# Row sums of a 64 MB tensor: the first group loaded as 4 and 12 rows, and a one-column copy ahead of the last sum

## The chip, the cores and the metric

One core of a Trainium2 chip. The time is device time in microseconds (us) of one execution; the profile's span is about 1.86 us shorter.

## The reference

```python
def setup_inputs():
    batch, seq, dim = 32, 512, 1024
    return {"x": np.random.randn(batch, seq, dim).astype(np.float32)}

def reference(x):
    return np.sum(x, axis=-1).astype(np.float32)
```

16,384 rows of 1,024 floats are summed: 67.11 MB read, 64 KB written.

## The kernel before

Each of the 128 partitions takes 128 rows, in 8 groups of 16. A full group's load gives a partition 16 rows that lie together in memory (64 KB). VectorE sums most rows. Towards the end ScalarE takes some rows of each load. The very last row comes in two pieces, of 560 and 464 columns: the sum of the first piece is written in front of the second, so that the second piece's instruction gives the row's whole sum. `hold` makes one instruction wait for another: the third load, and behind it all later loads, is issued only when the first sum is done.

```python
    last = J // BIG - 1                 # BIG = 16, J = 128
    FIRST = 7
    pieces = (560, 464)
    # ... pools: "in" has 3 buffers of one group each
        def halves(dst, src):           # sum of a row: left half + right half, accumulated
            n = src.shape[-1] // 2
            return nc.vector.tensor_tensor_reduce(
                out=src[:, :n], in0=src[:, :n], in1=src[:, n:], scale=1.0, scalar=0.0,
                op0=mybir.AluOpType.add, op1=mybir.AluOpType.add, accum_out=dst)
    # ... rows(t, a, n, j, n_act, pairs): loads n rows from row j of each partition's share, sums
    #     n - n_act of them on VectorE (one reduction, or `halves` row by row), n_act on ScalarE
        j = last * BIG
        t = inpool.tile([P, BIG * dim + 4], fp32)
        rows(t, 0, FIRST, j, 0)         # 7 rows of the last group come first
        first = sums_of[-1]
        for g in range(last):
            t = inpool.tile([P, BIG * dim + 4], fp32)
            if g < last - 1:
                load = rows(t, 0, BIG, g * BIG, 0)
            else:
                rows(t, 0, BIG, g * BIG, 7, pairs=True)
            if g == 1:
                hold(load, first, "no descriptors of later loads while the first ones start")
        t = inpool.tile([P, BIG * dim + 4], fp32)
        rows(t, FIRST, 6, j + FIRST, 2, pairs=True)
        two = rows(t, FIRST + 6, 2, j + FIRST + 6, 1, pairs=True)
        # ... the two pieces of the last row are loaded into `part` and `whole`
        hold(store(nc.scalar, 0, last), two, "its packets come behind those of the loads")
        halves(whole[:, :1], part)
        halves(sums[:, j : j + 1], whole)
        store(nc.sync, last, last + 1)
```

Of the kernel before, what the change touches and what calls it, by code (L numbers as in the profile page):

```python
# [118 lines left out]
@with_exitstack  # L119
def kernel(  # L120
    ctx: ExitStack,
    tc: tile.TileContext,
    x: bass.AP,
    out: bass.AP,
):
    nc = tc.nc
    nc.at_finalize(issue_first_load_at_entry)
    nc.at_finalize(order_waits)
    nc.at_finalize(wait_for_the_store_at_the_clear)
    fp32 = mybir.dt.float32  # L130
    P = 128
    batch, seq, dim = x.shape
    rows = batch * seq
    J = rows // P
    BIG = 16


    x_g = x.flatten_outer_dims().rearrange("(g p j) d -> g p j d", p=P, j=BIG)
    out_v = out.rearrange("b s -> (b s)").rearrange("(g p j) -> p g j", p=P, j=BIG)

    def rows_from(j, n):
        return x_g[j // BIG, :, j % BIG : j % BIG + n, :]



    last = J // BIG - 1
    FIRST = 7
    pieces = (560, 464)

    with (  # L150
        tc.tile_pool(name="in", bufs=3) as inpool,
        tc.tile_pool(name="unread", bufs=4, space=bass.MemoryType.PSUM) as upool,
        tc.tile_pool(name="stage", bufs=1) as stpool,
        tc.manual_schedule(),
    ):
        sums = stpool.tile([P, J], fp32)

        def vec(dst, src):
            return nc.vector.tensor_reduce(  # L159
                out=dst, in_=src, axis=mybir.AxisListType.X, op=mybir.AluOpType.add  # L160
            )

        def hold(inst, until, reason):
            tc.add_manual_dep(
                inst.ins,
                until.ins.name,
                mybir.DependencyInfo(mybir.DependencyClass.Sync, mybir.DependencyReason.DATA),
                reason=reason,
            )

        def halves(dst, src):
            n = src.shape[-1] // 2
            return nc.vector.tensor_tensor_reduce(  # L173
                out=src[:, :n],
                in0=src[:, :n],
                in1=src[:, n:],
                scale=1.0,
                scalar=0.0,
                op0=mybir.AluOpType.add,
                op1=mybir.AluOpType.add,  # L180
                accum_out=dst,
            )

        def act(dst, src, n):
            unread = upool.tile([P, dim], fp32)
            nc.scalar.activation(  # L186
                out=unread[:, :n],
                in_=src,
                func=mybir.ActivationFunctionType.Copy,
                accum_out=dst,  # L190
            )

        sums_of = []

        def rows(t, a, n, j, n_act, pairs=False):
            nv = n - n_act
            block = t[:, a * dim : (a + n) * dim].rearrange("p (n d) -> p n d", d=dim)
            load = nc.sync.dma_start(out=block, in_=rows_from(j, n))  # L198
            if pairs:
                for q in range(nv):  # L200
                    sums_of.append(halves(sums[:, j + q : j + q + 1], block[:, q, :]))
            else:
                sums_of.append(vec(sums[:, j : j + nv], block[:, :nv, :]))
            for q in range(nv, n):
                act(sums[:, j + q : j + q + 1], block[:, q, :], dim)
            return load

        def store(eng, g0, g1):
            return eng.dma_start(
                out=out_v[:, g0:g1],  # L210
                in_=sums[:, g0 * BIG : g1 * BIG].rearrange("p (g j) -> p g j", j=BIG),
            )


        j = last * BIG
        t = inpool.tile([P, BIG * dim + 4], fp32)
        rows(t, 0, FIRST, j, 0)
        first = sums_of[-1]
        for g in range(last):
            t = inpool.tile([P, BIG * dim + 4], fp32)  # L220
            if g < last - 1:
                load = rows(t, 0, BIG, g * BIG, 0)
            else:
                rows(t, 0, BIG, g * BIG, 7, pairs=True)
            if g == 1:
                hold(load, first, "no descriptors of later loads while the first ones start")

        t = inpool.tile([P, BIG * dim + 4], fp32)
        rows(t, FIRST, 6, j + FIRST, 2, pairs=True)
        two = rows(t, FIRST + 6, 2, j + FIRST + 6, 1, pairs=True)  # L230
        a = BIG - 1



        j += a
        c, width = pieces
        whole = t[:, a * dim + c : BIG * dim + 2]
        nc.vector.memset(whole[:, width + 1 :], 0.0)  # L238
        part = t[:, a * dim : a * dim + c]
        nc.sync.dma_start(out=part, in_=rows_from(j, 1)[:, 0, :c])  # L240
        nc.sync.dma_start(out=whole[:, 1 : width + 1], in_=rows_from(j, 1)[:, 0, c:])
        hold(store(nc.scalar, 0, last), two, "its packets come behind those of the loads")
        halves(whole[:, :1], part)
        halves(sums[:, j : j + 1], whole)
        store(nc.sync, last, last + 1)


# [28 lines left out]
```

## Time and profile before

| | before |
|---|---|
| time, median of the first 3 runs | 161.63 us (161.49 to 162.1) |
| span of the profile | 159.57 us |
| queue of the loads | 12 loads, busy 97.8% |
| VectorE, ScalarE busy | 76%, 7% |
| last load lands / last sum starts / last store issued | 157.51 / 157.57 / 158.01 us |

How to read it: the loads fill the span, so what can be gained is a quicker start of the stream, less overhead in it, or a shorter tail after the last landing. The lines are in the prediction. One view more, VectorE's timeline at the end of the kernel before (start, duration, engine, line, operation, operands): the first piece's sum (280 pairs), the read-out of its accumulator, and the second piece's sum (233 pairs).

```profile
156.97 0.45 DVE L173 CUSTOM_DVE_ANT_0 t<-t 128x280 f32<-128x280 f32 x1
157.34 0.08 DVE L173 DVE_READ_ACCUMULATOR2_ANT t<- 128x1 f32 x1
157.57 0.41 DVE L173 CUSTOM_DVE_ANT_0 t<-t 128x233 f32<-128x233 f32 x1
```

Between the read-out's end (157.42) and the start at 157.57 VectorE does nothing.

### The profile page before, as it was taken

The page shows a single profiled execution, that of the slowest core. Times are in us where ns is not written, and L with a number is a line of the kernel's source. Part 1 is how long each engine was busy: PE and PEld are TensorE (multiplying, and loading weights), DVE is VectorE, ACT ScalarE, POOL GpSimd, SP SyncE. Part 2 cuts the span into 40 slices and gives each one's busy share as a digit, 9 for nine tenths or more (in the row PEclk, how much of TensorE's full clock was granted, in tenths as well). Part 3 has the DMA queues.
Part 4 walks back from the last instruction along what each step waited for, and adds up shares of the span by engine and source line. Part 5 has one row for each costly group of instructions (what it writes and reads, how often), then busy time and mean ns, then how long its engine had stood idle before and what let it go on. Part 6 is the DMA issues. An engine that isn't in the chain of part 4 may idle for free.

```text
span 159.6 us, 134 instructions
## 1 busy us (share of the span) xinstructions
DVE 120.6 (76%) x40; ACT 11.9 (7%) x21; POOL 0.2 (0%) x4
## 2 busy tenths in 40 slices
DVE  0029600499995999779996899949999499994955
ACT  3000000000000000000000000000000000002993
POOL 0000000000000000000000000000000000000000
DMA  8899899799699699699699799998996996996994
GB/s 323 367 493 526 378 411 526 312 476 526 263 526 526 263 526 526 263 526 493 296 526 444 345 526 394 394 526 378 411 526 279 509 526 263 526 526 265 425 382 127
DMA packets 2784, 67.18 MB, mean 421 GB/s; under 512 B 1248, under 2 KB 1376, under 8 KB 1504
## 3 DMA queue, kind: packets, MB, share of 16 engines
q1 hardware_dynamic: 1872, 67.12, 97.8%
q10 hardware_dynamic: 912, 0.06, 0.4%
HBM read 67.11 MB, written 0.07 MB: 421 GB/s over the span
## 4 chain that ended last, share of the span: by engine, by line
DMA 71%; DVE 27%; SPq 1%; issue 0%; DVEq 0%
DMA t<-in_x_dram 71%; DVE sums L159 26%; SPq L198 0%; SPq L240 0%; DVE t L173 0%; DVEq L271 0%
## 5 line engine op out<-in xcount | busy, mean ns | idle before, releaser
L159 DVE TENSOR_REDUCE sums<-t 128x16 f32<-128x16384 f32 (+1 forms) x7 | 110.9, 15848 | 33.3 <-DMA t<-in_x_dram 33.3
L186 ACT ACTIVATE unread<-t 128x1024 f32<-128x1024 f32 x10 | 10.1, 1013 | 144.7 <-DMA t<-in_x_dram 144.7
L173 DVE CUSTOM_DVE_ANT_0 t<-t 128x512 f32<-128x512 f32 (+2 forms) x16 | 9.7, 656 | 4.0 <-DMA t<-in_x_dram 3.8
L186 ACT ACTIVATION_READ_ACCUMULATOR unread<-t 128x1 f32 x10 | 1.9, 187 | 0.0
L186 ACT ACT_TABLE_LOAD x1 | 1.3, 1283 | 0.8 <-PEq L260 0.8
L173 DVE DVE_READ_ACCUMULATOR2_ANT sums<- 128x1 f32 x15 | 1.2, 83 | 0.0
L260 POOL MEMSET const-bfloat16-1.0<- 128x1 bf16 x1 | 0.1, 101 | 0.0
L260 POOL MEMSET const-uint8-127<- 128x1 uint8 x1 | 0.1, 101 | 0.0
L260 POOL MEMSET const-float32-0.0<- 128x1 f32 x1 | 0.1, 98 | 0.2 <-issue 0.2
L260 POOL MEMSET const-float32-1.0<- 128x1 f32 x1 | 0.1, 98 | 0.0
L173 DVE DVE_READ_ACCUMULATOR2_ANT t<- 128x1 f32 x1 | 0.1, 81 | 0.0
L238 DVE MEMSET t<- 128x1 f32 x1 | 0.1, 59 | 0.0
## 6 DMA issues: line engine op xcount, KB each, us to landing
t<-in_x_dram SPq DMA_DIRECT2D x1, 3584.0 KB, 11.0
t<-in_x_dram SPq DMA_DIRECT2D x1, 3072.0 KB, 28.7
t<-in_x_dram SPq DMA_DIRECT2D x1, 1024.0 KB, 30.9
t<-in_x_dram SPq DMA_DIRECT2D x1, 280.0 KB, 31.1
t<-in_x_dram SPq DMA_DIRECT2D x1, 232.0 KB, 31.2
t<-in_x_dram SPq DMA_DIRECT2D x7, 40.8
out_dram<-sums ACTq DMA_DIRECT2D x1, 56.0 KB, 2.1
out_dram<-sums SPq DMA_DIRECT2D x1, 8.0 KB, 1.4
```

Of the source, the lines that this page charges most:

```text
L159: return nc.vector.tensor_reduce(out=dst, in_=src, axis=mybir.AxisListType.X, op=mybir.AluOpType.add)
L173: return nc.vector.tensor_tensor_reduce(out=src[:, :n], in0=src[:, :n], in1=src[:, n:], scale=1.0, scalar=0.0, op0=mybir.AluOpType.add, op ...
L186: nc.scalar.activation(out=unread[:, :n], in_=src, func=mybir.ActivationFunctionType.Copy, accum_out=dst,)
L238: nc.vector.memset(whole[:, width + 1 :], 0.0)
L260: nc = _bacc.Bacc("TRN2", target_bir_lowering=False, num_devices=1)
```

## The change

The intent: the last sum shall wait for its load alone. A one-column copy, which reads the first piece's sum, takes the wait for that sum; the last sum writes its unread output to a tile of its own. The order of the loads changes with it: the first group comes first, as 4 and 12 rows, and the last group at the end whole, as 8, 5, 2 and the two pieces.

```diff
-    FIRST = 7
+    FIRST = 4
...
+        seen = stpool.tile([P, 1], fp32)
+        scratch = stpool.tile([P, pieces[1]], fp32)
...
-        def halves(dst, src):
+        def halves(dst, src, unread=None):
...
-                out=src[:, :n],
+                out=src[:, :n] if unread is None else unread[:, :n],
...
-        j = last * BIG
-        t = inpool.tile([P, BIG * dim + 4], fp32)
-        rows(t, 0, FIRST, j, 0)
-        first = sums_of[-1]
         for g in range(last):
             t = inpool.tile([P, BIG * dim + 4], fp32)
-            if g < last - 1:
-                load = rows(t, 0, BIG, g * BIG, 0)
-            else:
-                rows(t, 0, BIG, g * BIG, 7, pairs=True)
+            if g == 0:
+                rows(t, 0, FIRST, 0, 0)
+                first = sums_of[-1]
+                rows(t, FIRST, BIG - FIRST, FIRST, 0)
+                continue
+            load = rows(t, 0, BIG, g * BIG, BIG // 2 if g == last - 1 else 0)
...
-        rows(t, FIRST, 6, j + FIRST, 2, pairs=True)
-        two = rows(t, FIRST + 6, 2, j + FIRST + 6, 1, pairs=True)
+        j = last * BIG
+        rows(t, 0, 8, j, 4)
+        rows(t, 8, 5, j + 8, 2, pairs=True)
+        two = rows(t, 13, 2, j + 13, 1, pairs=True)
...
         halves(whole[:, :1], part)
-        halves(sums[:, j : j + 1], whole)
+        nc.vector.tensor_copy(out=seen, in_=whole[:, :1])
+        halves(sums[:, j : j + 1], whole, unread=scratch)
```

## The prediction

> **What bounds the kernel now.** I read the page first: the line of VectorE, the queues and the chain.
>
> ```profile
> DVE 120.6 (76%) x40; ACT 11.9 (7%) x21; POOL 0.2 (0%) x4
> ...
> q1 hardware_dynamic: 1872, 67.12, 97.8%
> ...
> HBM read 67.11 MB, written 0.07 MB: 421 GB/s over the span
> ...
> DMA 71%; DVE 27%; SPq 1%; issue 0%; DVEq 0%
> ```
>
> VectorE is busy for 76% of the span, the queue of the loads for 97.8%. The chain gives 27% to VectorE, but a chain can run through a sum merely because that sum released a buffer. So I checked in VectorE's timeline whether loads ever wait for sums. Columns are start, duration, engine, line, operation, operands, and the idle time before it.
>
> ```profile
> 10.99 7.62 DVE L159 TENSOR_REDUCE sums<-t 128x7 f32<-128x7168 f32 x1 [10.99 <-DMA t<-in_x_dram]
> 30.31 17.22 DVE L159 TENSOR_REDUCE sums<-t 128x16 f32<-128x16384 f32 x1 [11.70 <-DMA t<-in_x_dram]
> 49.66 17.22 DVE L159 TENSOR_REDUCE sums<-t 128x16 f32<-128x16384 f32 x1 [2.13 <-DMA t<-in_x_dram]
> ...
> 127.06 17.22 DVE L159 TENSOR_REDUCE sums<-t 128x16 f32<-128x16384 f32 x1 [2.12 <-DMA t<-in_x_dram]
> 146.42 1.03 ACT L186 ACTIVATE unread<-t 128x1024 f32<-128x1024 f32 x1 [144.36 <-DMA t<-in_x_dram]
> ...
> 153.72 1.03 ACT L186 ACTIVATE unread<-t 128x1024 f32<-128x1024 f32 x1
> ...
> 156.24 1.03 ACT L186 ACTIVATE unread<-t 128x1024 f32<-128x1024 f32 x1 [0.33 <-DMA t<-in_x_dram]
> 156.24 0.69 DVE L173 CUSTOM_DVE_ANT_0 t<-t 128x512 f32<-128x512 f32 x1
> ```
>
> Each full group (16 rows a partition, 8.39 MB) starts its sum 19.35 us after the one before it, 19.32 after the first piece, with no gap that grows: the stream of loads never pauses, and each sum takes 17.22, so VectorE idles 2.1 us a group. The kernel is one stream of bytes, with a start (first piece) and a tail (after the last byte). The tail is the end of the chain in order of time:
>
> ```profile
> 126.30 31.21 DMA t<-in_x_dram
> 157.51 0.06 issue
> 157.57 0.41 DVE t L173
> 157.97 0.01 DVEq L271
> ```
>
> The last load lands at 157.51. Its instruction starts 0.06 later, where starts after other landings in this chain take 0.02 (a load lands at 10.96, the sum starts at 10.99). The last sum takes 0.41, then the last store is issued (158.01, lasting 0.35) and lands 1.4 us after that start. The time outside the trace's span is 161.43 - 159.6 = 1.8 us in the same run.
>
> **What the Trainium skill says.** "DMA: Bandwidth & Descriptors", section "Where 436 GB/s comes from", puts the ceiling of the 16 engines' ports at 435.2 GB/s. This trace agrees: 8.39 MB in 19.35 us is 433.5 GB/s, so nothing in the middle can gain. The same page, section "Why a DMA increments its semaphore by 16 and not by 1", says that each participating engine ends a load with a write to the semaphore. The packet count agrees: 12 loads and the last store make 13 transfers, and 13 x (128 + 16) = 1872. "Perfetto Trace Analysis", section "Identifying Dependency Chains", says an instruction with waits on several engines may have semaphore instructions put before it. The trace shows three of these for the line of the sums by halves, the last at 157.5, just ahead of the last sum:
>
> ```profile
> L173 DVEq EVENT_SEMAPHORE  x3: 21/21/21, 127.1 to 157.5; - x3
> ```
>
> "VectorE: DVE Perf Modes", section "The DRAIN you can't avoid", says that a read after a write on the same engine needs a semaphore or an instruction between. That is why the second piece's sum, which reads the first piece's sum as one of its elements, has that wait at all.
>
> **The change part by part.**
>
> *The wait taken off the last sum.* Before, VectorE's sequencer first meets the wait for the first piece's sum (a semaphore instruction of 0.02 at 157.46, since that sum's read-out ends at 157.34 + 0.08 = 157.42), and only then hands on the last sum, which starts at 157.57, about 0.08 after that instruction ended (157.48). The load had landed at 157.51. With the load's wait alone it would start about 0.02 after landing. Gain: 0.06 - 0.02 = 0.03 to 0.04 us, all of it on the path that sets the end.
>
> *The copy added.* One column; the memset of one column takes 0.06 (the one at 156.89), my estimate for the copy. It waits for the first piece's sum, so it starts about 157.42 + 0.03 = 157.45 and ends by 157.52 on the old clock. The load lands at 157.51. The copy is therefore beside the load by a hair; it may take back 0 to 0.04 of the gain.
>
> *One more load.* Before: 7, 16 x 7, 6, 2 rows and two pieces, 12 loads. After: 4, 12, 16 x 6, 8, 5, 2 rows and two pieces, 13 loads. What one load costs in a full stream comes from landings: 16 rows 19.35; 6 rows 153.72 - 146.42 = 7.30; so a row is (19.35 - 7.30) / 10 = 1.205 and a load 7.30 - 6 x 1.205 = 0.07. The two rows (156.24 - 153.72 = 2.52) give 0.11; the last row in two pieces (157.51 - 156.22 = 1.29, taking 0.02 off the start) gives 0.04 each. I take 0.07. It is on the path, because the stream is the path: +0.07 us.
>
> *The start.* The first load is issued at 0.00 in both, the second right behind it (10 issues of one line begin at 0.00). First landing: 10.96 - 3 x 1.205 = 7.35, and the 4-row sum takes 7.62 x 4/7 = 4.4, so the later loads held behind it are released at 11.8 instead of 18.6. By then the 12 rows behind run until 7.35 + 12 x 1.205 + 0.07 = 21.9, so the stream never lacks work, and it lacked none before. Worth 0.
>
> *VectorE and ScalarE in the tail.* Before the last group there are now 8 rows of a group for ScalarE (7 before), then 8 rows split 4 and 4, then 5, 2, 1. By 1.205 a row: the sixth full group lands at 127.03 - 7 x 1.205 = 118.6 (103 rows had landed at 127.03; now 96), its sum ends at 135.8; the next group lands at about 138.0, 8 rows on VectorE take 8.6 (17.22 / 2) to 146.6, and 8 on ScalarE take 8 x 1.04 = 8.3 to 146.3. The 8 rows of the last group land at 147.7: four on VectorE 4.4 to 152.1, four on ScalarE 4.2 to 151.9. The 5 rows land at 153.8: three by halves at 0.61 (starts 153.72 and 154.34 are 0.62 apart) end near 155.7; the 2 rows land at 156.3. Both engines are idle at each of the last landings. Before, VectorE was busy until 156.26 when the two rows had landed at 156.22, so up to 0.02 comes back, off the path. Worth 0.
>
> *Sum:* +0.07 - 0.035 + about 0.02 for the copy = +0.05 us. 161.63 + 0.05 = 161.68; I say 161.7.
>
> **The rivals.**
>
> *The copy takes the place of the wait.* For: by the times above it ends within 0.02 of the landing, and an instruction behind it must also get through the engine. Against: the extra load moves landing and copy together, so the margin stays. If it bound, the last sum would start 0.05 to 0.10 after landing, time 161.7 to 161.8.
>
> *The whole wait was worth more than it looks.* The ceiling is all that lies between landing and last sum's end, 0.46 us. Even that gone is 161.2, 0.3%.
>
> *A load exposes its fixed cost.* The skill's DMA page ("Anatomy of one DMA", a fixed part of about 2 us, described there for the GpSimd path) would make 163.6 if the extra load paid it in the stream. Against: the landings above show 0.07 a load with several loads queued.
>
> *The earlier release of held loads disturbs the 12 rows in flight.* Before, the same release came at 18.6 with 16 rows in flight, which landed after 19.35 - 0.03: no trace of harm.
>
> *A tail bound by compute.* If the 4-row reduction or ScalarE ran 1.7 us late, the end would move; the margins above (153.8 - 152.1) speak against it.
>
> **Range and chances.** Every term is under 0.1 us, far below the spread of the runs of before (161.49 to 162.1). So the range is that spread about my figure: 161.4 to 162.1. Over 2% is 3.2 us, more than all that follows the last landing in the span (159.6 - 157.5 = 2.1), and no term or rival reaches it: within 2% 0.98, 0.01 on each side.
>
> **What would show it right or wrong.** Right: 2016 packets on the loads' queue (14 x 144); VectorE's first sum at about 7.4 lasting 4.4, the second at about 21.9 lasting 13; starts 19.35 apart after it; the last load's landing 0.05 to 0.1 later than 157.51; 0.02 to 0.03 from landing to the last sum, and no semaphore instruction before it. Wrong: a landing earlier than 157.45, a full group's spacing other than 19.35, a last sum held by the copy, or a start of the stream that changes with the size of the first load.

## The result and the profile after

The changed kernel: 161.63 us median of 6 runs (161.38 to 162.16), the kernel before 161.70 in 6 runs (161.49 to 162.1). The ratio is 0.9997, with a 95% interval of 0.9974 to 1.002: the same. Ratios here are the mean time of one kernel's fast runs over that of the other's of the same rounds, so not quite the ratio of the medians.

The queue and the chain on the page of the changed kernel:

```profile
q1 hardware_dynamic: 2016, 67.12, 97.8%
...
DMA 73%; DVE 25%; SPq 0%; issue 0%; DVEq 0%
```

2016 packets are the 14 transfers (13 loads and a store) of 144 that the prediction named. VectorE's timeline of the changed kernel:

```profile
7.25 4.42 DVE L161 TENSOR_REDUCE sums<-t 128x4 f32<-128x4096 f32 x1 [7.25 <-DMA t<-in_x_dram]
21.77 12.95 DVE L161 TENSOR_REDUCE sums<-t 128x12 f32<-128x12288 f32 x1 [10.11 <-DMA t<-in_x_dram]
41.12 17.22 DVE L161 TENSOR_REDUCE sums<-t 128x16 f32<-128x16384 f32 x1 [6.40 <-DMA t<-in_x_dram]
...
99.17 17.22 DVE L161 TENSOR_REDUCE sums<-t 128x16 f32<-128x16384 f32 x1 [2.13 <-DMA t<-in_x_dram]
...
118.73 17.22 DVE L161 TENSOR_REDUCE sums<-t 128x16 f32<-128x16384 f32 x1 [2.34 <-DMA t<-in_x_dram]
...
138.43 8.69 DVE L161 TENSOR_REDUCE sums<-t 128x8 f32<-128x8192 f32 x1 [2.47 <-DMA t<-in_x_dram]
...
157.55 0.45 DVE L175 CUSTOM_DVE_ANT_0 t<-t 128x280 f32<-128x280 f32 x1
...
157.92 0.08 DVE L175 DVE_READ_ACCUMULATOR2_ANT t<- 128x1 f32 x1
158.04 0.15 DVE L247 COPY seen<-t 128x1 f32<-128x1 f32 x1
158.12 0.40 DVE L175 CUSTOM_DVE_ANT_0 scratch<-t 128x233 f32<-128x233 f32 x1
```

Three things are to be seen. The first two landings (7.22 and 21.75; each sum starts 0.02 to 0.03 later) are 0.13 to 0.15 us earlier than the prediction's 7.35 and 21.9. Then the groups come 19.35 apart, but two come late: 99.17 to 118.73 is 19.56, and 118.73 to 138.43 is 19.70. The packets of these groups took longer themselves (up to 2.66 us for 64 KB, against the usual 2.42), and VectorE sat idle longer ahead of them (2.34, 2.47), and the loads of both groups had been issued over 40 us ahead of their landings; so neither a sum nor an empty queue held the stream up. At the end, the last load's completion is recorded at 158.100 and the last sum starts at 158.123, 0.023 later; before it was 157.512 and 157.567, 0.055. No semaphore instruction stands at the last sum any more; the one left is at 148.2:

```profile
L175 DVEq EVENT_SEMAPHORE  x1: 21/21/21, 148.2 to 148.2; - x1
```

So the profile of after has a longer span (160.1) than that of before (159.6) although its tail is shorter, because of the late groups. Of its six times three lie at 161.38 and 161.39 and three at 161.88 to 162.16. What is worth a few hundredths must therefore be read from the parts of each trace, not from the time.

### The profile page after: what moved, and what is told of

It reads as the page before. It is cut to its first block, busy times and chain, and to the rows that moved or that the text cites. A ratio compares the mean times of both kernels' runs of the same rounds, so it can differ in the third digit from the quotient of the medians.

```text
span 160.1 us, 127 instructions
## 1 busy us (share of the span) xinstructions
DVE 120.2 (75%) x23; ACT 17.3 (11%) x31; POOL 0.2 (0%) x4
## 3 DMA queue, kind: packets, MB, share of 16 engines
q1 hardware_dynamic: 2016, 67.12, 97.8%
## 4 chain that ended last, share of the span: by engine, by line
DMA 73%; DVE 25%; SPq 0%; issue 0%; DVEq 0%
DMA t<-in_x_dram 73%; DVE sums L161 24%; DVE t L175 1%; SPq L200 0%; DVE scratch L175 0%; DVE seen L247 0%; DVE t L239 0%; DVE sums L175 0%; DVEq L275 0%
## 5 line engine op out<-in xcount | busy, mean ns | idle before, releaser
L161 DVE TENSOR_REDUCE sums<-t 128x16 f32<-128x16384 f32 (+3 forms) x9 | 116.6, 12953 | 36.1 <-DMA t<-in_x_dram 36.1
L188 ACT ACTIVATE unread<-t 128x1024 f32<-128x1024 f32 x15 | 15.2, 1014 | 139.9 <-DMA t<-in_x_dram 139.9
L175 DVE CUSTOM_DVE_ANT_0 t<-t 128x512 f32<-128x512 f32 (+1 forms) x5 | 3.1, 643 | 2.3 <-DMA t<-in_x_dram 2.3
L188 ACT ACTIVATION_READ_ACCUMULATOR unread<-t 128x1 f32 x15 | 2.8, 189 | 0.0
L175 DVE DVE_READ_ACCUMULATOR2_ANT sums<- 128x1 f32 x5 | 0.4, 83 | 0.0
```

Of the source, the lines that this page charges most:

```text
L161: return nc.vector.tensor_reduce(out=dst, in_=src, axis=mybir.AxisListType.X, op=mybir.AluOpType.add)
L175: return nc.vector.tensor_tensor_reduce(out=src[:, :n] if unread is None else unread[:, :n], in0=src[:, :n], in1=src[:, n:], scale=1.0, sc ...
L188: nc.scalar.activation(out=unread[:, :n], in_=src, func=mybir.ActivationFunctionType.Copy, accum_out=dst,)
```

## The experiments

Theory: the wait's removal gains 0.035 us, one load more costs 0.07, the start is worth nothing. Rivals: the copy binds; the size of the first load changes the start; a load costs nothing, or much more.

In what follows, "wait" is the last sum's start minus the last load's completion, and "tail" is the span's end minus that completion.

### The copy alone

The kernel before, with the copy and the separate output.

```diff
-        halves(sums[:, j : j + 1], whole)
+        nc.vector.tensor_copy(out=seen, in_=whole[:, :1])
+        halves(sums[:, j : j + 1], whole, unread=scratch)
```

> The kernel before with the copy and the separate output alone; its 12 loads stay. My theory: the last sum starts 0.02 to 0.03 us after the last landing (0.055 before), everything else as before, so about 0.03 us less time, which the spread of runs will hide (ratio 0.998 to 1.002). Rival, that the copy binds: the last sum starts 0.05 us or more after the landing.

161.59 us (161.41 to 161.83), ratio 0.9998 (0.9985 to 1.0012). Its end, where the copy starts at 157.75 and the sum 0.07 later:

```profile
157.63 0.08 DVE L175 DVE_READ_ACCUMULATOR2_ANT t<- 128x1 f32 x1
157.75 0.15 DVE L246 COPY seen<-t 128x1 f32<-128x1 f32 x1
157.82 0.40 DVE L175 CUSTOM_DVE_ANT_0 scratch<-t 128x233 f32<-128x233 f32 x1
```

Wait 0.029 us (157.794 to 157.823): 0.026 off the 0.055, as expected. It is 0.006 above the 0.023 of after, so here the copy itself is what the sum waits for, by a hair: the sum starts 0.071 after the copy, as in four other traces (0.070 to 0.071).

### The loads alone

The changed kernel without the copy and the separate output.

```diff
-        nc.vector.tensor_copy(out=seen, in_=whole[:, :1])
-        halves(sums[:, j : j + 1], whole, unread=scratch)
+        halves(sums[:, j : j + 1], whole)
```

> The changed kernel without the copy: its 13 loads alone. My theory: a semaphore instruction stands again before the last sum, which starts 0.05 to 0.07 us after the landing; one load more makes it about 0.07 us slower than the kernel before, if the start is worth nothing. Rival, that the smaller first load starts the stream earlier: the first full group of 16 rows lands 0.1 us earlier than 10.96 + 1.205 us a row would have it, and the time is equal to before or less.

161.52 us (161.37 to 161.54), ratio 0.9991 (0.9978 to 1.0004). Its chain again ends with the longer wait, and its trace has a semaphore instruction at 157.6 again:

```profile
157.62 0.06 issue
157.68 0.40 DVE t L173
...
L173 DVEq EVENT_SEMAPHORE  x2: 21/21/21, 147.6 to 157.6; - x2
```

Wait 0.059. So the copy with its separate output, and nothing in the loads, takes the wait away; no run has one of the two without the other, so what each does alone is not shown. But this kernel isn't 0.07 slower than before. Its 16 first rows have landed for a sum at 21.74, where the kernel before gives 30.31 - 7 x 1.205 = 21.87: in this trace the start is earlier, as the rival has it, and the prediction's step "worth 0" is in doubt.

### The changed kernel again

> The changed kernel once more, unaltered. In its first profile two groups in the middle were 0.21 and 0.35 us late against the usual 19.35, and three of its six times were 161.4, three 161.9 to 162.2. If that lateness is a disturbance that comes and goes, this profile either lacks it (span about 159.5) or has it elsewhere, and the times fall again in two clusters about 0.5 us apart. If it belongs to this kernel, the same two groups are late by the same amount.

161.59 us (161.40 to 161.91), ratio 0.9999 (0.9983 to 1.0015). Spacings 19.35 to 19.36 up to the completion at 118.56, then 19.56 for the next group and 9.85 for 8 rows (9.71 in an undisturbed trace). So lateness comes again, but smaller and beginning a group later: it doesn't belong to a fixed place. The times don't make two clear clusters this time (161.40, 161.46, 161.47, 161.71, 161.87, 161.91). Wait 0.022.

### A copy 512 columns wide

```diff
-        seen = stpool.tile([P, 1], fp32)
+        seen = stpool.tile([P, 512], fp32)
...
-        nc.vector.tensor_copy(out=seen, in_=whole[:, :1])
+        nc.vector.tensor_copy(out=seen, in_=t[:, a * dim + c : a * dim + c + 1].broadcast_to([P, 512]))
```

> The changed kernel with the copy made 512 columns wide (the one column repeated), so that it surely ends after the last landing. If the copy lies within 0.02 us of binding, as I predicted, the last sum starts later by nearly the whole width of the copy: 0.3 us or more after the landing instead of 0.023, and the span grows by as much. If the engine had 0.2 us or more to spare there, under 0.1 us would show.

161.55 and 161.67 us, ratio 0.9999 (0.9978 to 1.0019): 0.25 us is not to be seen in two times, only in the trace.

```profile
157.25 0.08 DVE L175 DVE_READ_ACCUMULATOR2_ANT t<- 128x1 f32 x1
157.37 0.43 DVE L247 COPY seen<-t 128x512 f32<-128x512 f32 x1
157.71 0.40 DVE L175 CUSTOM_DVE_ANT_0 scratch<-t 128x233 f32<-128x233 f32 x1
```

Wait 0.275 us instead of 0.022: 0.25 later, just under the 0.3 that I named. The sum follows this copy's start by 0.34, the one-column copy's by 0.07 where the copy is what it waits for, and the copy is recorded as 0.43 and 0.15: in both the next instruction starts 0.08 to 0.09 ahead of the recorded end. The tail grew from 2.01 to 2.25. The copy stands at the edge of the path: one column has no room to grow.

### Fifteen loads more

```diff
-            load = rows(t, 0, BIG, g * BIG, BIG // 2 if g == last - 1 else 0)
+            if g == last - 1:
+                rows(t, 0, BIG, g * BIG, BIG // 2)
+                continue
+            load = rows(t, 0, 4, g * BIG, 0)
+            for a in range(4, BIG, 4):
+                rows(t, a, 4, g * BIG + a, 0)
```

> The changed kernel with five of its full groups loaded and summed in quarters of 4 rows: 15 loads more. My theory, 0.07 us a load in a full stream: each of these groups takes 0.2 us longer (19.55 instead of 19.35), the time grows by 1.05 us to about 162.5. Rival, that a load costs nothing beyond its bytes: no growth. Rival, that a load exposes a fixed 2 us: 30 us more.

162.50 us (162.44 to 162.56), ratio 1.0059 (1.0047 to 1.0072).

```profile
100.04 4.42 DVE L161 TENSOR_REDUCE sums<-t 128x4 f32<-128x4096 f32 x1 [0.48 <-DMA t<-in_x_dram]
104.93 4.42 DVE L161 TENSOR_REDUCE sums<-t 128x4 f32<-128x4096 f32 x1 [0.47 <-DMA t<-in_x_dram]
109.82 4.42 DVE L161 TENSOR_REDUCE sums<-t 128x4 f32<-128x4096 f32 x1 [0.48 <-DMA t<-in_x_dram]
```

Each quarter comes 4.89 to 4.90 after the last. The twenty quarters take 119.592 - 21.672 = 97.92 us, where five groups of 19.35 are 96.75: 1.17 / 15 = 0.078 us a load. VectorE waits for every quarter (0.48), so it isn't what slows them. The step "one load more, 0.07" holds.

### One row first

```diff
-    FIRST = 4
+    FIRST = 1
```

> The changed kernel with the first group loaded as 1 and 15 rows. My prediction (the size of the first load is worth nothing): 16 rows have landed at 21.75, as with 4 and 12. Rival, that a smaller first load starts the stream earlier, which the profiles so far hint at (16 rows at 21.68 to 21.79 with 4 first, 21.85 to 21.92 worked out with 7 first): 21.6 or less.

161.75 us (161.71 to 161.93), ratio 1.0018 (1.0004 to 1.0032).

```profile
22.16 16.15 DVE L161 TENSOR_REDUCE sums<-t 128x15 f32<-128x15360 f32 x1 [17.21 <-DMA t<-in_x_dram]
```

16 rows at 22.13: neither my 21.75 nor the rival's 21.6. The first row lands at 3.70 and the 15 others 18.43 later, where 15 x 1.205 + 0.08 makes 18.15. All later groups are regular (19.34 to 19.37), so the 0.38 lost at the start against 21.75 stays to the end. Wait 0.031.

### Seven rows first, twice

```diff
-    FIRST = 4
+    FIRST = 7
```

> The changed kernel with the first group loaded as 7 and 9 rows: the size of the kernel before, at the address of the changed one. If the size of the first load makes the earlier start, 16 rows have landed at 21.85 to 21.92. If the place in memory does (the kernel before begins with the last group), they have landed at 21.68 to 21.79.

162.12 and 161.94 us, ratio 1.0031 (1.0012 to 1.0049); 16 rows at 22.06, later than both bands, so against the place in memory and beyond what the size was expected to do.

> The changed kernel with 7 and 9 rows once more, timed in more rounds. If its later start (16 rows at 22.06 in the first look) belongs to the sizes, 16 rows land at 22.0 to 22.1 again and the fastest run is about 0.3 us above 161.38. If it was chance, 16 rows land anywhere from 21.7 to 22.1.

162.00 us (161.88 to 162.31), ratio 1.003 (1.0018 to 1.0042); 16 rows at 21.94. So the later start is there again, though 0.06 outside the narrow band expected, and the fastest run is 0.5 above 161.38, not 0.3. The rest comes from late groups, five of them in this profile (completions 19.43 to 19.60 apart). The sum of the 9 rows, and two of the late groups, in VectorE's timeline:

```profile
21.97 9.75 DVE L161 TENSOR_REDUCE sums<-t 128x9 f32<-128x9216 f32 x1 [3.41 <-DMA t<-in_x_dram]
...
80.23 17.22 DVE L161 TENSOR_REDUCE sums<-t 128x16 f32<-128x16384 f32 x1 [2.21 <-DMA t<-in_x_dram]
99.79 17.22 DVE L161 TENSOR_REDUCE sums<-t 128x16 f32<-128x16384 f32 x1 [2.33 <-DMA t<-in_x_dram]
119.27 17.22 DVE L161 TENSOR_REDUCE sums<-t 128x16 f32<-128x16384 f32 x1 [2.26 <-DMA t<-in_x_dram]
```

### Twelve rows first

```diff
-    FIRST = 4
+    FIRST = 12
```

> The changed kernel with the first group loaded as 12 and 4 rows. If the start loses with the size of the first load, 16 rows have landed later than with 7 and 9: after 21.9. If only the first packets' start matters and not their size, at 21.7 to 21.9.

172.25 and 172.96 us, ratio 1.0685 (1.0661 to 1.0709). The 16 rows land at 21.92, 0.02 beyond the 21.9 that parts the two theories and not later than with 7 and 9 (21.94 to 22.06), so it doesn't tell them apart. It shows something that I hadn't put down: the hold. The chain of this run:

```profile
0.00 17.04 DMA t<-in_x_dram
17.06 12.96 DVE sums L161
30.04 21.94 DMA t<-in_x_dram
```

The later loads wait for the sum of the first 12 rows, which ends at 30.02. The stream ran dry at 21.9. Once released, a full group takes 21.94 us instead of 19.35: refilling the stream costs 2.6. With 4 rows first the release comes at 11.7, ten microseconds ahead of need.

### Four rows of the last group first

The kernel before with FIRST = 4, its last 12 rows as 4, 5, 2 and 1.

```diff
-    FIRST = 7
+    FIRST = 4
...
-        rows(t, FIRST, 6, j + FIRST, 2, pairs=True)
-        two = rows(t, FIRST + 6, 2, j + FIRST + 6, 1, pairs=True)
+        rows(t, 4, 4, j + 4, 2, pairs=True)
+        rows(t, 8, 5, j + 8, 2, pairs=True)
+        two = rows(t, 13, 2, j + 13, 1, pairs=True)
```

> The kernel before with 4 rows of the last group loaded first in place of 7 (the 12 others as 4, 5, 2 and 1 at the end, so 13 loads; no copy). If the size of the first load sets the start, the first landing is at 7.2, as with 4 rows of the first group, not at 10.96 - 3 x 1.205 = 7.35, and the first full group of 16 rows lands 19.33 later, at 26.5. If the place in memory does, 7.35 and 26.7. In time 0.07 for the load more, so 161.5 or 161.6 in runs without a late group.

161.64 us (161.44 to 161.81), ratio 1.0003 (0.9991 to 1.0014).

```profile
7.20 4.42 DVE L159 TENSOR_REDUCE sums<-t 128x4 f32<-128x4096 f32 x1 [7.20 <-DMA t<-in_x_dram]
26.55 17.22 DVE L159 TENSOR_REDUCE sums<-t 128x16 f32<-128x16384 f32 x1 [14.93 <-DMA t<-in_x_dram]
```

7.17 and 26.52 as completions: the earlier start goes with the size of the first load, not with its place in memory. Wait 0.054, with no copy, as before.

### Two rows first

```diff
-    FIRST = 4
+    FIRST = 2
```

> The changed kernel with 2 and 14 rows first. If the loss at 1 and 15 rows (16 rows at 22.13) comes from a first load so short that the second is still starting when the first is over, 2 rows (2.4 us of stream, over at about 4.5) are free of it and 16 rows land at 21.7 to 21.8. If 4 and 12 are a lucky pair of sizes, 2 and 14 land at 21.9 or later.

162.08 us (161.69 to 162.29), ratio 1.0028 (1.0013 to 1.0043). 16 rows at 21.51, better than both expectations, and then the 0.24 gained against 21.75 is given back five times over (0.70 + 0.50):

```profile
21.53 15.09 DVE L161 TENSOR_REDUCE sums<-t 128x14 f32<-128x14336 f32 x1 [14.64 <-DMA t<-in_x_dram]
41.57 17.22 DVE L161 TENSOR_REDUCE sums<-t 128x16 f32<-128x16384 f32 x1 [4.96 <-DMA t<-in_x_dram]
61.43 17.22 DVE L161 TENSOR_REDUCE sums<-t 128x16 f32<-128x16384 f32 x1 [2.63 <-DMA t<-in_x_dram]
80.75 17.22 DVE L161 TENSOR_REDUCE sums<-t 128x16 f32<-128x16384 f32 x1 [2.10 <-DMA t<-in_x_dram]
```

The next two groups come 20.04 and 19.86 apart, then 19.32.

### Without the hold

```diff
             if g == 1:
-                hold(load, first, "no descriptors of later loads while the first ones start")
+                pass
```

> The changed kernel without the hold of the later loads behind the first sum. The prediction took the moment of that release as worth nothing: then 16 rows land at 21.75 and the times are those of the changed kernel. Rival, that descriptors of later loads disturb the start: 16 rows land 0.1 us or more later.

161.88 us (161.31 to 162.13), ratio 1.0022 (1.001 to 1.0035). 16 rows at 21.66: the moment of the release is worth nothing at the start, as predicted. The times don't follow the expectation: the interval of the ratio lies above 1, where the changed kernel's two (in other rounds) include 1. The profiled run, 161.31, is the fastest, and it has no late group: spacings 19.35 to 19.36 throughout, span 159.44, wait 0.024, tail 2.009. The five other runs are 0.4 to 0.8 slower, and their traces weren't kept. So whether the hold makes late groups rarer stays open.

## Why the prediction was right

The time was right (161.7 predicted, 161.63 measured, well inside 161.4 to 162.1), and its chances too. But the sum of its terms came to +0.05 us, and the traces show a sum of about -0.1 with one term wrong. The size of both lies below what the times can tell. The hit is therefore no test of the terms: the range is the scatter of the kernel before, and any sum from about -0.2 to +0.5 would have fallen into it.

| term | predicted | shown by |
|---|---|---|
| wait off the last sum | -0.035 | wait 0.054 to 0.059 without the copy (3 traces) and 0.022 to 0.031 with it (10 traces with the one-column copy): -0.03, net of what the copy takes back |
| the copy | +0.02 | 0 in the changed kernel (0.023 after landing), up to 0.008 in others (0.031), already in the line above |
| one load more | +0.07 | 1.17 us for 15 loads: +0.078 |
| the start | 0 | about -0.14, see below |
| VectorE and ScalarE in the tail | 0 | both idle at the landings of the 5 rows and the 2 rows: 0 |

**The wait** went as told: the semaphore instruction is gone, and the sum follows its landing as others do. The traces show what the sum waited for. In all three without the copy it starts 0.144 after the end of the first piece's read-out (157.423 to 157.567 in the kernel before) and 0.084 after the end of the semaphore instruction, so it was held by that wait and not by the load, which had landed 0.054 to 0.059 earlier. The copy starts 0.034 to 0.035 after the read-out's end, and where the copy holds the sum, that starts 0.105 to 0.106 after it. The tail went from 2.059 to 2.009 between these two profiles; over all traces it is 2.042 to 2.059 without the copy and 2.006 to 2.016 with the one-column copy, 0.04 between the means.

**The copy** was mis-sized but its verdict held. I took 0.06 from the memset; it is recorded as 0.15. What matters to the next instruction is the 0.07 after its start at which that one could begin. "Perfetto Trace Analysis" of the Trainium skill, section "Optimizing Scalar/DVE Operations", gives a data-access overhead of about 60 ns of engine time for each instruction of VectorE on SBUF and says that the profiled latency is about twice that, since the write's acknowledgement overlaps with the next instruction. These traces agree for a copy of one column, with 0.07 and 0.15. The rival "the copy takes the place of the wait" fell in the changed kernel with 0.023, but only just: in five traces of its variants and of the copy alone the copy does hold the sum, by up to 0.008, and the wide copy shows that added length comes straight onto the path.

**The step that failed is the start, "worth 0".** The prediction asked only whether the stream would lack work, and took the rest of the start to be the same whatever the size of the first load. (The row of 10 issues that it read at 0.00 is a merged one: the second load is issued at 0.78, in both kernels.) It scaled the first landing by rows (10.96 - 3 x 1.205 = 7.35). Seven traces with 4 rows first have it at 7.14 to 7.27; four with 7 rows have 10.91 to 11.03. For the same 39 rows in 3 loads the kernel before has 49.63 (completion) and the changed one's third load, 32 rows at 41.10, plus 7 x 1.205 makes 49.54; over six traces, which are regular up to there, the difference is 0.05 to 0.23, 0.14 between the means (before and the copy alone against the changed kernel, its repeat, the loads alone and the wide copy).

Four rows of the last group behave as four of the first, so it is the size. It holds on each of the three chips: 16 rows at 21.68 to 21.79 against 21.92 (worked out) on chip 14, 21.67 against 22.06 on chip 12, 21.66 against 21.94 on chip 6. The packed traces part the 0.14 further. They have a completion for each of the 16 DMA engines, and the last of them is the landing. By the mean of the 16, the third load is earlier by 0.05; the other 0.09 is that the last engine lags less behind the mean (0.16 to 0.29 in the four traces, 0.27 to 0.34 in the two).

It isn't simply "smaller is earlier": 16 rows have landed at 22.13 with 1 and 15, 21.51 with 2 and 14, 21.66 to 21.79 with 4 and 12, 21.94 to 22.06 with 7 and 9, 21.92 with 12 and 4. Why is not shown by these runs.

So three of the prediction's four signs of being wrong came up. The start changes with the size of the first load. In the two profiles without a late group and with the changed kernel's loads (the wide copy, no hold) the last load lands at 157.44 and 157.43, before its 157.45. And groups came 19.56 and 19.70 apart instead of 19.35, which is the lateness below and none of its terms. The other rivals fell: a load costs 0.078 and not 2 us, the 12 rows in flight at the release took 14.53 (14.49 without the hold), and neither engine was late in the tail.

**The sum.** -0.14 for the start, +0.08 for the load, -0.04 for the tail make -0.10. The nearest check is a pair of undisturbed traces: the kernel before has a span of 159.57, the changed kernel without the hold 159.44, which is 0.13 less.

**Why none of it is in the time.** A gain of 0.1 us is 0.06%, and the interval of the ratio is 0.23% wide to each side. Late groups are larger than the gain: 0.6 and 0.35 us in the changed kernel's two profiles, none in the one profile of before. Late groups show in the kernel before with the copy too (completions up to 19.46 apart), and most with 2 or 7 rows first. They come with longer packets and not with a queue that is empty, and not at a fixed group. What makes them, and whether the sizes of the first loads decide how often they come, stays open: one trace a run is too few to count them.

No version beat both kernels beyond doubt. The copy alone, which keeps 12 loads, has ratio 0.9998; the loads alone 0.9991, and its interval includes 1. Besides 12 rows first and the 15 loads, four variants of the start are slower than the kernel before by 0.2 to 0.3%, with intervals above 1: 1, 2 and 7 rows first, and no hold.

## What to carry to other kernels

When a stream of loads sets the time, split the argument into start, cost of each load, and tail, and read each from completions in the trace: terms of 0.03 to 0.15 us are plain there and lost in times that scatter by 0.6. A wait that stands in a semaphore instruction of its own ahead of the last instruction can be moved onto a cheap instruction before it (here together with a separate output for the last one), as long as that one ends before the other wait does. A load that is held behind the sum of an earlier one is safe only while that sum ends before the queued bytes do; where it didn't, the stream ran dry and cost 10.7 us (8.1 dry, from 21.92 to 30.04, and 2.6 to refill).

## What the Trainium skill lacked or had wrong

- "DMA: Bandwidth & Descriptors": the cost of one load more in a stream that never pauses. Here it is 0.078 us for loads of 2 MB over 128 partitions; the fixed part of about 2 us in "Anatomy of one DMA", told of the GpSimd path, shows, for these loads issued from SP, only where the stream is empty: at its start (10.96 - 7 x 1.205 = 2.5 us) and where it ran dry (2.6 us to refill it).
- The same page: that the size of the first load moves the start of the whole stream. 16 rows landed between 21.51 and 22.13 us by how they were cut. No page has it.
- The same page: late stretches of a full stream. Groups of 8.39 MB took 19.35 us, at times 19.4 to 20.0, with 64 KB packets of up to 2.75 us (2 rows first) in place of 2.42. I found them on no page.
- "VectorE: DVE Perf Modes", section "The DRAIN you can't avoid": the page measured a row of copies and says that the semaphore "costs nothing extra here". For an instruction that also waits for a load it is not so here: the wait stood in a semaphore instruction of its own, and the last sum started 0.144 us after the read-out that it waited for, where the copy, which carries the same wait itself, started 0.034 to 0.035 after it.
